# Halving the work pieces of rows 4 to 7 and re-cutting the last loads of a row-wise squared-distance kernel

## The chip, the cores and the metric

The kernel runs on one core of a Trainium2 chip. Times are device microseconds (us) of whole executions. A trace is one profiled execution; its span is some 1.9 us shorter than the time of the same execution (83.5 against 85.35 us for the profiled run before), and all positions below are microseconds from the start of the span.

## The reference

```python
batch, dim = 1024, 4096          # x, y: float32
def reference(x, y, axis):       # axis = -1
    return np.sum((x - y) ** 2, axis=axis).astype(np.float32)
```

## The kernel before

Each of the 128 partitions holds 8 rows of 4096 columns, so 32768 columns of x and as many of y pass through it. VectorE (DVE) subtracts in place, ScalarE (ACT) squares in place and sums along the columns through its accumulator. SyncE (SP) issues the loads. Buffers hold six rows; rows 6 and 7 come into the place of rows 0 and 1 and wait until those are squared.

The sizes of the loads (columns per partition; the late piece is the end of row 3, kept for the very last):

```python
xw = [16384, 8192, 5568, 1824, 512, 288]
yw = [16224, 8192, 2656, 2912, 928, 896, 512]
late, last = 160, 288
```

The loop runs over the y loads. A load is cut only at row borders, each piece is subtracted on VectorE and squared on ScalarE, and the piece that lands last is squared on VectorE itself:

```python
for j, (c0, c1) in enumerate(ys):
    final = j == len(ys) - 1
    wait_loaded(c1, landed_y[j][1])
    # ... pieces: [c0, c1) cut at multiples of D ...
    for piece in pieces:
        sub(*piece)                         # VectorE, X -= Y
        if final:
            # ... tensor_tensor_reduce on VectorE, starting from row 3's sum ...
            continue
        square(*piece, where[piece])        # ScalarE, waits for the subtraction
        # ... issue of rows 6 and 7 once rows 0 and 1 are squared ...
    if j == 4:
        complete(6)                         # VectorE adds the partial sums of row 6
complete(7)
```

## Time and profile before

| | before |
|---|---|
| time, median of 3 | 85.19 us (85.11 to 85.19) |
| span of the trace | 83.5 us |
| VectorE busy | 36.3 us, 18 instructions |
| ScalarE busy | 31.7 us, 27 instructions |
| loads | 15, 33.55 MB read, mean 402 GB/s |

The loads fill most of the span, so the kernel is near the pace of its data. The two compute engines look idle, at 44 and 38%, but that is an average: over 40 us they wait for the first large load, and in the last 10 us both are busy nearly all the time. The question for a change at the end of the kernel is which of the two, or which load, ends last there. The prediction shows the chain and the last instructions and reads them.

The group of subtractions and the group of squares, from the page of the kernel before (columns: line, engine, operation, output from input, shapes, count, then total busy us and mean ns of one, then idle time before them and what ended it):

```profile
L165 DVE TENSOR_TENSOR X<-X,Y 128x4096 f32<-128x4096 f32 (+9 forms) x14 | 35.8, 2593 | 45.2 <-DMA Y<-in_y_dram 45.1
L171 ACT ACTIVATE X<-X 128x4096 f32<-128x4096 f32 (+8 forms) x13 | 29.7, 2287 | 48.0 <-DVE X L165 48.0
L171 ACT ACTIVATION_READ_ACCUMULATOR X<-X 128x1 f32 x13 | 2.4, 186 | 0.0
```

ScalarE waits only for VectorE, VectorE only for loads, and every square has a second instruction of 186 ns behind it that reads the accumulator. Back to back, a square takes 0.185 us more than its columns (0.61 us for 512 columns, of which 0.427 are columns), so cutting squares in pieces is not free.

### The profile page before, as it was taken

Reading aid. Unit: us, or ns where it says so; the run is one execution under the profiler, and the core shown is the slowest. Engines: PE = TensorE matmul, PEld = TensorE weight load, DVE = VectorE, ACT = ScalarE, POOL = GpSimd, SP = SyncE. Lnnn points to the kernel's source line nnn. Section 1 sums busy time; section 2 is a strip of 40 time slices with the busy share of each in tenths; the row PEclk is TensorE's granted clock in tenths of the full one; section 3 lists DMA queues with packets and bytes.
Section 4 is the critical chain, followed back from the end, with each engine's and each line's share of the span. In section 5 each row is a group of like instructions: output and inputs, shape, how many; then the busy total and the mean of one; then the engine's idle time right before and its main releaser. Section 6 shows DMA issues by size and latency. Waiting matters only on the chain.

```text
span 83.5 us, 109 instructions
## 1 busy us (share of the span) xinstructions
DVE 36.3 (44%) x18; ACT 31.7 (38%) x27; POOL 0.2 (0%) x4
## 2 busy tenths in 40 slices
DVE  0000000000000000000299999999099995979980
ACT  0500000000000000000001979697970897989990
POOL 0000000000000000000000000000000000000000
DMA  9389999956999999589989998997999899999920
GB/s 471 157 377 502 502 502 502 471 251 283 497 497 497 497 497 404 218 373 497 439 377 439 487 439 345 487 487 330 423 437 437 378 443 427 423 407 410 394 66 2
DMA packets 2305, 33.56 MB, mean 402 GB/s; under 512 B 385, under 2 KB 769, under 8 KB 1409
## 3 DMA queue, kind: packets, MB, share of 16 engines
q1 hardware_dynamic: 2304, 33.56, 94.7%
q14 instruction: 1, 0.00, 0.0%
HBM read 33.55 MB, written 0.00 MB: 402 GB/s over the span
## 4 chain that ended last, share of the span: by engine, by line
DMA 68%; ACT 14%; DVE 14%; SPq 1%; issue 0%
DMA Y<-in_y_dram 68%; ACT X L171 14%; DVE X L165 14%; SPq L108 1%; DVE results L178 0%; SPq L215 0%
## 5 line engine op out<-in xcount | busy, mean ns | idle before, releaser
L165 DVE TENSOR_TENSOR X<-X,Y 128x4096 f32<-128x4096 f32 (+9 forms) x14 | 35.8, 2593 | 45.2 <-DMA Y<-in_y_dram 45.1
L171 ACT ACTIVATE X<-X 128x4096 f32<-128x4096 f32 (+8 forms) x13 | 29.7, 2287 | 48.0 <-DVE X L165 48.0
L171 ACT ACTIVATION_READ_ACCUMULATOR X<-X 128x1 f32 x13 | 2.4, 186 | 0.0
L171 ACT ACT_TABLE_LOAD x1 | 1.3, 1283 | 1.9 <-PEq L19 1.9
L178 DVE TENSOR_REDUCE results<-parts 128x1 f32<-128x2 f32 (+1 forms) x2 | 0.3, 152 | 0.2 <-ACT X L171 0.2
L199 DVE CUSTOM_DVE_ANT_0 Y<-X,parts 128x160 f32<-128x160 f32 x1 | 0.4, 385 | 0.0
L244 POOL MEMSET const-bfloat16-1.0<- 128x1 bf16 x1 | 0.1, 101 | 0.0
L244 POOL MEMSET const-uint8-127<- 128x1 uint8 x1 | 0.1, 101 | 0.0
L244 POOL MEMSET const-float32-0.0<- 128x1 f32 x1 | 0.1, 98 | 0.2 <-issue 0.2
L244 POOL MEMSET const-float32-1.0<- 128x1 f32 x1 | 0.1, 98 | 0.0
L199 DVE DVE_READ_ACCUMULATOR2_ANT results<- 128x1 f32 x1 | 0.1, 83 | 0.0
## 6 DMA issues: line engine op xcount, KB each, us to landing
Y<-in_y_dram SPq DMA_DIRECT2D x1, 8112.0 KB, 40.7
X<-in_x_dram SPq DMA_DIRECT2D x1, 4096.0 KB, 48.9
Y<-in_y_dram SPq DMA_DIRECT2D x1, 4096.0 KB, 58.3
X<-in_x_dram SPq DMA_DIRECT2D x1, 2784.0 KB, 13.4
Y<-in_y_dram SPq DMA_DIRECT2D x1, 1456.0 KB, 19.2
Y<-in_y_dram SPq DMA_DIRECT2D x1, 1328.0 KB, 16.2
X<-in_x_dram SPq DMA_DIRECT2D x1, 912.0 KB, 21.0
Y<-in_y_dram SPq DMA_DIRECT2D x1, 464.0 KB, 21.6
```

Of the source, the lines that this page charges most:

```text
L108: nc.sync.dma_start(out=dst[:, home(c0, c1)], in_=src[:, c0:c1]).then_inc(sem, 16)
L165: nc.vector.tensor_sub(out=a, in0=a, in1=Y[:, home(c0, c1)]).then_inc(diffs, 1)
L171: nc.scalar.activation(out=a, in_=a, func=Square, accum_out=acc).then_inc(acts, 1)
L178: nc.vector.tensor_reduce(out=results[:, r : r + 1], in_=parts_of(r, len(row_parts[r])), axis=mybir.AxisListType.X, op=add,).then_inc(sums, 1)
L199: nc.vector.tensor_tensor_reduce(out=Y[:, home(*piece)], in0=X[:, home(*piece)], in1=X[:, home(*piece)], scale=1.0, scalar=parts_of(r, 1), ...
L244: nc = _bacc.Bacc("TRN2", target_bir_lowering=False, num_devices=1)
```

## The change

The intent is to let ScalarE start on the first half of a piece while VectorE subtracts the second, and to bring the last data in smaller and more even portions. The edit, shortened where a line begins with @@, and without blank lines:

```diff
-    xw = [16384, 8192, 5568, 1824, 512, 288]
-    yw = [16224, 8192, 2656, 2912, 928, 896, 512]
-    late, last = 160, 288
+    xw = [16384, 8192, 5472, 1280, 960, 320, 160]
+    yw = [16256, 8192, 2624, 2784, 1344, 480, 480, 288]
+    late, last = 128, 192
     LATE = 3
+    halved = (1, 2, 3, 4)
@@ pieces are now cut by one function, used for the partial sums too @@
+    def pieces_of(j, c0, c1):
+        pieces = []
         while c0 < c1:
             e = min(c1, (c0 // D + 1) * D)
-            row_parts[c0 // D].append((c0, e))
+            if j in halved:
+                h = (c0 + e) // 64 * 32
+                pieces.append((c0, h))
+                c0 = h
+            pieces.append((c0, e))
             c0 = e
+        return pieces
@@ in the loop @@
         if j == 4:
-            complete(6)
+            for r in (4, 5, 6):
+                complete(r)
```

Load 1 is rows 4 and 5, load 2 the first 2624 columns of row 6, load 3 the next 2784 (the end of row 6 and the start of row 7), load 4 the next 1344; these four are halved per row. A row squared in several pieces has several partial sums, so rows 4 and 5 now need a `complete` of their own, a short reduction on VectorE.

More of the change, by code (lines that the diff above doesn't have):

```diff
@@ L127 @@
     row_parts = [[] for _ in range(R)]
-    for c0, c1 in ys:
+    def pieces_of(j, c0, c1):
+        pieces = []
         while c0 < c1:
             e = min(c1, (c0 // D + 1) * D)
-            row_parts[c0 // D].append((c0, e))
+            if j in halved:
[3 more added lines that the diff above has]
+            pieces.append((c0, e))
             c0 = e
+        return pieces
+    for j, (c0, c1) in enumerate(ys):
+        for piece in pieces_of(j, c0, c1):
+            row_parts[piece[0] // D].append(piece)
     parts, where = None, {}
@@ L188 @@
         wait_loaded(c1, landed_y[j][1])
-        pieces = []
-        while c0 < c1:
-            e = min(c1, (c0 // D + 1) * D)
-            pieces.append((c0, e))
-            c0 = e
-        for piece in pieces:
+        for piece in pieces_of(j, c0, c1):
             sub(*piece)
```

## The prediction

> **What bounds the kernel now.** I read the chain that ended last first, then the table of loads with their times to landing, then the last eight microseconds instruction by instruction, and the groups by shape for the cost of one instruction. The chain in order of time ends so:
>
> ```profile
> 54.11 16.24 DMA Y<-in_y_dram
> 70.35 0.02 issue
> 70.37 2.94 DVE X L165
> 73.31 0.02 issue
> 73.33 8.28 ACT X L171 x14
> 81.61 0.02 issue
> 81.64 0.16 DVE results L178
> ```
>
> Columns: start, duration, what. Up to 70.35 us the kernel waits for loads. From then on one whole subtraction (2.94 us, 2656 columns of row 6) lies on the chain, and behind it seven squares on ScalarE with their accumulator reads, back to back. So the end is not set by the last load but by a ScalarE that began row 6 late. The page's share of 68% for DMA hides this; the last 11 us are compute. The last instructions:
>
> ```profile
> 80.47 0.61 ACT L171 ACTIVATE X<-X 128x512 f32<-128x512 f32 x1
> 80.99 0.19 ACT L171 ACTIVATION_READ_ACCUMULATOR X<-X 128x1 f32 x1
> 81.02 0.39 DVE L199 CUSTOM_DVE_ANT_0 Y<-X,parts 128x160 f32<-128x160 f32 x1
> 81.08 0.43 ACT L171 ACTIVATE X<-X 128x288 f32<-128x288 f32 x1
> 81.33 0.08 DVE L199 DVE_READ_ACCUMULATOR2_ANT results<- 128x1 f32 x1
> 81.41 0.19 ACT L171 ACTIVATION_READ_ACCUMULATOR X<-X 128x1 f32 x1
> 81.64 0.16 DVE L178 TENSOR_REDUCE results<-parts 128x1 f32<-128x5 f32 x1 [0.23 <-ACT X L171]
> ```
>
> The last bracket is the point: VectorE waits 0.23 us for ScalarE before the final reduction. ScalarE's backlog is thus worth only about 0.2 to 0.3 us, because VectorE itself is done at 81.41. The loads (KB, us from issue to landing):
>
> ```profile
> Y<-in_y_dram SPq DMA_DIRECT2D x1, 1328.0 KB, 16.2
> ...
> Y<-in_y_dram SPq DMA_DIRECT2D x1, 464.0 KB, 21.6
> ...
> Y<-in_y_dram SPq DMA_DIRECT2D x1, 80.0 KB, 15.4
> ```
>
> With the issue times (54.11, 55.58, 65.07) these land at 70.3, 77.2 and 80.5. All landings after rows 4 and 5 (60.6) found in this way are 67.1, 70.3, 73.8, 76.1, 77.2, 78.2, 78.9, 79.5, 79.9, 80.3, 80.5 for 2784, 1328, 1456, 912, 464, 448, 256, 256, 144, 144 and 80 KB. A line through the steps between them gives 2.35 us per 1000 KB (436 GB/s) and 0.04 us per load, and meets every landing within 0.1 us. The queue does not run dry between the batches: the second batch is issued at 53.7, while the first runs to 60.6.
>
> **What the Trainium skill says.** "ScalarE: Activation LUTs", Rules for kernel authors, gives some 0.3 us per ACTIVATE and 0.83 ns per element. The trace agrees in slope (3617 ns for 4096 columns, 2417 for 2656: 0.833 ns), but back to back the fixed part is smaller: 512 columns go from 80.47 to the next start at 81.08, 0.61 us, less 0.427 is 0.185. "VectorE: DVE Perf Modes", Specifications and Mode 1×, gives one result per cycle at 0.96 GHz, 1.042 ns; the trace has (4421 - 2925)/1440 = 1.039 ns, with 0.155 us fixed, of which 0.08 overlap the next instruction, so 0.075 per extra subtraction. "DMA: Bandwidth & Descriptors", Bandwidth, calls transfers under 64 KB descriptor-dominated; the smallest new load is 64 KB, and here an 80 KB load behind others landed 0.2 us after its predecessor, so I price it by the fit. The same page, Queues, rings and completion order, has each DMA engine consume its ring in order; the landings above are in order of issue.
>
> **The change, part by part.** Nothing before 60.6 us changes except that the first y load has 32 columns (16 KB, 0.04 us) more, so the second batch is issued some 0.04 us later into a queue that is full anyway. The bytes are the same; there are 13 loads instead of 11 after the first four, two more at 0.04 us, so the last landing moves from 80.47 to about 80.5. By the fit the new landings that gate a subtraction are 70.2 (row 6, first 2624), 73.5 (2784), 76.7 (1344), 78.4 and 79.0 (480 each), 79.8 (288), 80.3 (192), 80.5 (128).
>
> Halves add six subtractions (rows 4 and 5 one each; one in 24576 to 27200; two in 27200 to 29984, which spans rows 6 and 7; one in 29984 to 31328), the new sizes one more (the last loads give 480, 480, 288, 192 where 896, 512, 288 were), and as many squares. On VectorE that is 7 x 0.075 = 0.5 us, nearly all in gaps that it waits out for loads. On ScalarE it is 7 x 0.185 = 1.3 us of work.
>
> What they buy is the lag. Row 5's last square starts after half a row: VectorE ends the four halves at 60.59 + 4 x 2.21 + 0.08 = 69.5, ScalarE squares the last 2048 columns in 1.71 + 0.185, so it is free at 71.4 instead of 73.1. Row 6's first 1312 columns are subtracted 70.20 to 71.72, the square starts at 71.76 (0.035 us from one engine to the other, as 73.29 to 73.33 now) instead of 73.33: 1.57 us earlier. From there the work left is 8192 columns as before, 6.83 us, but in 12 squares instead of 7: 12 x 0.185 = 2.22 instead of 1.30. Without any wait it would end at 71.76 + 9.05 = 80.81; so 0.92 of the 1.57 goes to fixed cost. Waits for subtractions come in between. Going through the pieces, each starting when its subtraction is done and the square before it is: 1312 at 71.76 and 73.20; 736 at 74.47 and 75.31; 640 at 76.10; 672 at 76.82, 77.59 and 78.37; 480 at 79.15 and 79.74; 288 at 80.34; 192 at 80.77, its accumulator read at 81.2. Now it is 81.60. The same rule, applied to the kernel before, gives 81.57, so it is good to some hundredths.
>
> VectorE: the two extra reductions (rows 4 and 5) cost 0.07 us each in pitch (78.23 to 78.30 now), beside the wait for the 480 columns. Then sub 192 at 80.34, sub 128 at 80.61 to 80.90, the squared sum 0.035 later to 81.29 (0.385 less 32 columns, plus the read), and the final reduction at 81.30 to 81.45, where it now ends at 81.80. Sum: -0.3 us. ScalarE, at 81.2, no longer holds the reduction; VectorE's own serial end after the last loads does. The store after it is unchanged.
>
> **The rivals.** First, the new sizes alone could be doing the work: the same walk with the new loads and no halves gives a reduction at 81.65, within 0.02 of now, and halves with the old sizes 81.75, slightly worse, for ScalarE then pays four more fixed costs and still meets the large 896 piece late. So neither pays alone; the pair does, which I believe because ScalarE is the bound in both. If ScalarE's fixed cost in small pieces is 0.21 and not 0.185, the gain shrinks to 0.2 us: 85.0.
>
> Second, DMA takes what is won: smaller loads (80, 96, 64 KB at the end, rows of 512 to 768 bytes) could each cost 0.1 rather than 0.04. Against it: the 80 KB load with rows of 640 bytes fits the line. If it came true, the end moves 0.2 to 0.3 us and the time is 85.1 to 85.2: nothing won. Related: the queue takes only a limited number of loads, the issue of the 144 KB y load took 4.87 us and the last 2.77. Two more loads mean that the last is issued only at some 71 to 74 us, still 5 us or more before its turn, so I count nothing.
>
> Third, the three reductions after the subtraction of 31328 hold VectorE if one of them waits for ScalarE: row 6's last square should end at 76.1, two microseconds before. If they did wait, VectorE would start the 480s late and all of it shift by that wait, to 85.2 or more.
>
> **Range and chances.** 85.19 - 0.3 = 84.88. The runs of before spread by 0.1%; the walk is good to 0.05, the landings to 0.1, and the rest of the range is small-load cost on the high side and on the low side a ScalarE that waits less or loads that land earlier. 84.6 to 85.15. Two per cent is 1.7 us: a gain of that size would need an end before the last load lands, so faster by 2% is out of reach; slower by 2% would need a stall of 1.7 us that nothing shows.
>
> **What would show it.** Right: last square's read ends before VectorE's last squared sum, the wait of the final reduction for ScalarE is gone or under 0.1; row 6's first square starts at about 71.8; the last y load lands at 80.5 +- 0.1; the final reduction starts near 81.3 and the span is 83.2. Wrong: last landing at 80.7 or later (the load rival), a wait of VectorE for ScalarE before the reductions of rows 4 to 6 (third rival), or ScalarE back to back into the final reduction (fixed cost mis-sized).

## The result

The changed kernel took 84.91 us (median of 4, 84.87 to 85.03) where the kernel before took 85.16 (median of 4). Ratios here and below are the mean time of one kernel's fast runs over the mean of the other's fast runs of the same rounds, so they are not quite the ratio of the medians: 0.9974, with a 95% interval of 0.9956 to 0.9991. It is a gain of 0.25 us where 0.3 was predicted.

The page of the changed kernel, busy times and the same groups:

```profile
DVE 36.8 (44%) x27; ACT 33.4 (40%) x41; POOL 0.2 (0%) x4
...
L177 DVE TENSOR_TENSOR X<-X,Y 128x2048 f32<-128x2048 f32 (+10 forms) x21 | 36.2, 1779 | 44.4 <-DMA Y<-in_y_dram 44.3
L183 ACT ACTIVATE X<-X 128x2048 f32<-128x2048 f32 (+9 forms) x20 | 31.2, 1560 | 45.8 <-DVE X L177 45.7
L183 ACT ACTIVATION_READ_ACCUMULATOR X<-X 128x1 f32 x20 | 3.7, 187 | 0.0
```

The kernel became faster while both engines became busier: seven more subtractions and squares, ScalarE 1.7 us more in busy time. What fell is ScalarE's wait for VectorE, from 48.0 to 45.7 us.

The chain of work that ended last, its end, in the changed kernel (start, duration, what; "issue" is time in which the engine waited for nothing that the profile shows, x2 that two instructions are merged):

```profile
67.52 12.66 DMA Y<-in_y_dram
80.19 0.02 issue
80.21 0.57 DVE X L177 x2
80.78 0.03 issue
80.81 0.35 DVE Y L206
81.16 0.01 DVE results L206
81.17 0.14 DVE results L190
```

Before, this chain left the loads at 70.35 us and ran 8.3 us on ScalarE. Now it stays with the loads until 80.19, the landing of the 192 columns, and has one microsecond of VectorE behind it. That landing only just decides: VectorE was busy with the 288 columns until 80.19 too, and waited 0.01 us for the 192 (0.07 and 0.09 in the other two traces of the change). ScalarE is gone from the end. The last instructions, in order of time:

```profile
80.67 0.35 ACT L183 ACTIVATE X<-X 128x192 f32<-128x192 f32 x1
80.81 0.35 DVE L206 CUSTOM_DVE_ANT_0 Y<-X,parts 128x128 f32<-128x128 f32 x1
80.92 0.19 ACT L183 ACTIVATION_READ_ACCUMULATOR X<-X 128x1 f32 x1
81.08 0.08 DVE L206 DVE_READ_ACCUMULATOR2_ANT results<- 128x1 f32 x1
81.14 0.16 DVE L190 TENSOR_REDUCE results<-parts 128x1 f32<-128x8 f32 x1
```

The final reduction has no bracket any more: it does not wait for ScalarE, whose last read ends at 81.11, before VectorE's own at 81.17. The margin is small: 0.06 us here, 0.08 and 0.09 in the other two traces. The reduction starts at 81.14 instead of 81.64. That is 0.5 us in these two traces, more than the 0.25 us of the clocked runs, because the first load happened to land 0.13 us earlier in this trace (41.01 against 41.14), and because single executions scatter: the profiled run before took 85.35 us, above all four clocked ones, and the one after 84.87. Counted from that landing, the final reduction starts after 40.13 us instead of 40.50, a gain of 0.37. This count, "first subtraction to final reduction", is used for all traces below. It takes out the spread of the first landing, though not that of the later ones, and it is one execution for each line of the table, so small differences are judged by the ratios.

### The profile page after: what moved, and what is told of

Read it like the earlier page. It is cut to its first block, busy times and chain, and to the rows that moved or that the text cites. A ratio compares the mean times of both kernels' runs of the same rounds, so it can differ in the third digit from the quotient of the medians.

```text
span 83.0 us, 135 instructions
## 1 busy us (share of the span) xinstructions
DVE 36.8 (44%) x27; ACT 33.4 (40%) x41; POOL 0.2 (0%) x4
## 4 chain that ended last, share of the span: by engine, by line
DMA 64%; SPq 17%; DVE 12%; ACT 4%; issue 1%
DMA Y<-in_y_dram 64%; SPq L109 17%; DVE X L177 11%; ACT X L183 4%; DVE Y L206 0%; DVE results L190 0%; SPq L222 0%; DVE results L206 0%
## 5 line engine op out<-in xcount | busy, mean ns | idle before, releaser
L177 DVE TENSOR_TENSOR X<-X,Y 128x2048 f32<-128x2048 f32 (+10 forms) x21 | 36.2, 1779 | 44.4 <-DMA Y<-in_y_dram 44.3
L183 ACT ACTIVATE X<-X 128x2048 f32<-128x2048 f32 (+9 forms) x20 | 31.2, 1560 | 45.8 <-DVE X L177 45.7
L183 ACT ACTIVATION_READ_ACCUMULATOR X<-X 128x1 f32 x20 | 3.7, 187 | 0.0
```

The lines of the kernel that those rows point to most:

```text
L177: nc.vector.tensor_sub(out=a, in0=a, in1=Y[:, home(c0, c1)]).then_inc(diffs, 1)
L183: nc.scalar.activation(out=a, in_=a, func=Square, accum_out=acc).then_inc(acts, 1)
```

## The experiments

My theory was that the end is a race between ScalarE's queue of squares and VectorE's short tail behind the last load, so that the parts do not add up: every place where ScalarE is late must be mended at once. The runs below come from three calls, each with its own runs of the kernel before. The rivals were that the load sizes do it (A), that the parts add up (B), that small loads cost more than the fit says (C), and that ScalarE has slack (D). All eleven runs gave correct results.

| run | ratio to before (95%) | first subtraction to final reduction | last wait of VectorE for ScalarE |
|---|---|---|---|
| before | 1 | 40.50 | 0.23 |
| the change | 0.9974 (0.9956 to 0.9991) | 40.13 | none |
| the change, second time | 0.9966 (0.9954 to 0.9977) | 40.11 | none |
| the change, third time | 0.9959 (0.9935 to 0.9983) | 40.13 | none |
| new sizes, no halves | 1.0014 (0.9995 to 1.0033) | 40.63 | 0.30 |
| halves, old sizes | 1.0005 (0.9993 to 1.0017) | 40.64 | 0.31 |
| no halves in rows 4, 5 | 1.0063 (1.005 to 1.0075) | 41.04 | 0.85 |
| halves in rows 4, 5 only | 1.0018 (1.0005 to 1.0032) | 40.51 | 0.32 |
| the 1344 whole | 1.0017 (1.0005 to 1.0029) | 40.54 | 0.40 |
| the 480s halved too | 1.0004 (0.9991 to 1.0016) | 40.44 | 0.31 |
| three x loads cut | 0.9992 (0.998 to 1.0004) | 40.41 | none |
| the same, second time | 0.9979 (0.9953 to 1.0005) | 40.40 | none |
| seven more x loads | 1.0015 (0.9988 to 1.0041) | 40.49 | none |

### New sizes, no halves

```diff
-    halved = (1, 2, 3, 4)
+    halved = ()
-            for r in (4, 5, 6):
+            for r in (6,):
```

> The new load sizes without any halves. My theory (the end is a race of ScalarE's queue of squares against VectorE's tail, and only the pair of sizes and halves takes ScalarE out of it): ScalarE starts row 6 a whole 2624-column subtraction late again and is back to back into the final reduction; time within 0.15 us of the kernel before (walk: +0.06, 85.2). Rival A (smaller last loads and earlier landings do the work, the halves are idle): 84.9, the whole gain. Rival B (each part adds its share): 85.0 to 85.05.

Measured: 85.35 us beside 85.25 of the kernel before, ratio 1.0014. Rivals A and B, which wanted 84.9 and some 85.0, fall. The chain of this run has the shape of the kernel before:

```profile
70.12 2.90 DVE X L177
73.03 0.02 issue
73.05 8.54 ACT X L183 x16
81.58 0.02 issue
81.61 0.16 DVE results L190
```

One whole subtraction, then sixteen instructions of ScalarE back to back into the final reduction. The last load is not in it.

### Halves with the old sizes

```diff
-    xw = [16384, 8192, 5472, 1280, 960, 320, 160]
-    yw = [16256, 8192, 2624, 2784, 1344, 480, 480, 288]
-    late, last = 128, 192
+    xw = [16384, 8192, 5568, 1824, 512, 288]
+    yw = [16224, 8192, 2656, 2912, 928, 896, 512]
+    late, last = 160, 288
```

> Halves of the same four loads, with the old sizes. My theory: ScalarE is early until the 896, 512 and 288 columns, which come in large lumps, and has paid four more fixed costs by then; it still holds the final reduction: 0.1 us slower than the kernel before (85.25), a wait of VectorE for ScalarE of about 0.3 us at the end. Rival A (the sizes do it): 85.15, no change. Rival B (halves alone carry the gain because the lag is what matters): 84.9.

Measured: 85.29 us, ratio 1.0005: no gain, which refutes rival B, and the final reduction waits 0.31 us for ScalarE. The interval also admits rival A's "no change" for this run, but A has fallen in the first. From the end of the chain:

```profile
78.56 1.01 DVE X L177
79.57 0.02 issue
79.60 2.09 ACT X L183 x6
81.69 0.02 issue
81.71 0.16 DVE results L190
```

ScalarE has caught up by 79.3, waits 0.28 us until the whole 896 columns are subtracted, and from 79.60 has 896, 512 and 288 to square while VectorE finishes. The expectation named this lump.

### No halves in rows 4 and 5

```diff
-    halved = (1, 2, 3, 4)
+    halved = (2, 3, 4)
-            for r in (4, 5, 6):
+            for r in (6,):
```

> The change with rows 4 and 5 whole again (halves only in the loads of rows 6 and 7). My theory: ScalarE is still squaring row 5 until 72.9, so the halves of row 6 wait behind it; they add fixed cost and save no wait: 0.6 us slower than the kernel before (85.75), 0.9 slower than the change, ScalarE back to back from row 4 to the end. Rival B (parts add up): two thirds or more of the gain remain, 84.95 to 85.0. Rival A: 84.9.

Measured: 85.81 us, ratio 1.0063, 0.56 us slower than the kernel before and 0.8 slower than the change. This is the sharpest run: taking away one of four helpful-looking parts leaves a kernel that is worse than with none. The chain and the last line of the trace:

```profile
69.24 12.77 ACT X L183 x26
82.02 0.02 issue
82.04 0.16 DVE results L190
```

```profile
82.04 0.16 DVE L190 TENSOR_REDUCE results<-parts 128x1 f32<-128x8 f32 x1 [0.85 <-ACT X L183]
```

ScalarE starts on row 5 at 69.24 and has no pause for the remaining 12.77 us. Halves of row 6 arrive while it is still busy with row 5, so they only add their fixed cost.

### Halves in rows 4 and 5 only

```diff
-    halved = (1, 2, 3, 4)
+    halved = (1,)
```

> The new sizes, and halves in rows 4 and 5 only. My theory: ScalarE is free at 71.4 but then waits for a whole 2624-column subtraction until 73.1, so the time won is idle time: within 0.15 us of the kernel before (walk +0.06, 85.2). Rival B (parts add up): a third or more of the gain, 85.0 to 85.1. Rival A (sizes): 84.9.

Measured: 85.38 us beside 85.26, ratio 1.0018. No gain; rival B's third of it is outside the interval. ScalarE in this trace:

```profile
71.20 0.19 ACT L183 ACTIVATION_READ_ACCUMULATOR X<-X 128x1 f32 x1
73.03 2.39 ACT L183 ACTIVATE X<-X 128x2624 f32<-128x2624 f32 x1 [1.65 <-DVE X L177]
```

It is free at 71.4, as it is in the changed kernel, and then sits idle for 1.65 us, until a whole subtraction of 2624 columns is done. The time won on row 5 is given back as a wait.

### The load of 1344 columns whole

```diff
-    halved = (1, 2, 3, 4)
+    halved = (1, 2, 3)
```

> The change with the one load of 1344 columns whole again. My theory: ScalarE is idle until the whole 1344 are subtracted (78.1) and then has 1344, 480, 480, 288, 192 in its queue, which ends 0.35 us after VectorE: the whole gain is lost, +0.09 against the kernel before (85.25), with a wait of VectorE for ScalarE of 0.3 us before the last reduction. Rival B (parts add up): a quarter of the gain lost, 84.95 to 85.0.

Measured: 85.38 us, ratio 1.0017: the whole gain is gone with one half, where rival B wanted a quarter of it gone. The trace shows ScalarE waiting in the middle and VectorE at the end:

```profile
78.30 1.32 ACT L183 ACTIVATE X<-X 128x1344 f32<-128x1344 f32 x1 [0.60 <-DVE X L177]
```

```profile
81.69 0.16 DVE L190 TENSOR_REDUCE results<-parts 128x1 f32<-128x7 f32 x1 [0.40 <-ACT X L183]
```

Loads 2 and 3 were not left whole one at a time. An estimate: a walk by the prediction's rules on the landings in the changed kernel's trace, which meets the four runs with the new sizes and other sets of halves to within 0.06 us, puts the final reduction some 0.9 us later with load 2 whole and 0.3 us later with load 3 whole.

### The two loads of 480 columns halved as well

```diff
-    halved = (1, 2, 3, 4)
+    halved = (1, 2, 3, 4, 5, 6)
```

> The change with the two loads of 480 columns halved as well: two more squares of 0.185 us fixed cost. My theory: ScalarE becomes the bound of the end again by 0.25 us: 85.15, the last reduction waits for it. Rival D (only VectorE's tail counts, ScalarE has slack): 84.9 to 84.95.

Measured: 85.25 us, ratio 1.0004, 0.1 us above what I expected and 0.3 above the change by the ratios. Rival D falls: in the change ScalarE is done only 0.06 to 0.09 us before VectorE, and two more fixed costs are 0.37; the final reduction waits 0.31. Its chain ends with ScalarE again:

```profile
73.11 8.34 ACT X L183 x26
81.45 0.02 issue
81.48 0.16 DVE results L190
```

### More loads of the same bytes

The first of these cuts three x loads in two, and was run twice. The second makes seven more loads.

```diff
-    xw = [16384, 8192, 5472, 1280, 960, 320, 160]
+    xw = [16384, 8192, 5472, 640, 640, 480, 480, 160, 160, 160]                               # three more
+    xw = [16384, 8192, 5472, 320, 320, 320, 320, 240, 240, 240, 240, 160, 160, 160]           # seven more
```

> The change with three x loads cut in two (1280, 960, 320), nothing else. My theory: a load in a full queue costs 0.04 us, so the last landing and the end move by 0.12 us: 85.0 (84.97 to 85.08). Rival C (a small load costs 0.1 us or more, or the queue's limit on loads in it delays the last ones): 85.2 or more.

> The kernel with three x loads cut in two, unaltered, to see whether the 0.1 us before its first cut load comes back. If it was the spread of one run: 0.14 us above the change, first row-6 load landing 9.65 us after rows 4 and 5. If the cut loads cause it through their issue or their place in the queue: 0.22 us above and 9.75 us again.

> The change with its x loads of 1280 and 960 columns cut in four each and that of 320 in two: seven more loads, same bytes. The run with three cuts was 0.22 us slower than the change, of which its trace shows 0.14 us (0.047 us a load) between the landing of the 2784-column y load and the last but one y load, and 0.1 us before the first cut load. Theory 'a fixed 0.047 us a load in the full queue': the stretch from the landing of the 2784 columns to that of the 192 grows from 6.77 to 7.1 us, the time is 0.33 us above the change. Rival 'some 0.07 us or more a load, once the queue's limit holds back the last issues': 0.5 us or more above the change.

Measured: 85.19 us for three more loads, and 85.12 in the repetition; 85.4 for seven more. By the ratios that is 0.22, 0.17 and 0.48 us above the change measured in the nearest or the same call. My first expectation (0.12 us) was too low. By time alone the seven-load run leans to the rival (0.5 or more), but its interval is 0.45 us wide, so I read the traces. The stretch from the first subtraction of the 2784-column load to that of the 192 columns, both within 0.03 us of a landing, is 6.78, 6.80 and 6.83 us in the three traces of the change, 6.93 and 7.00 with three more loads, and 7.15 with seven more. Against their mean of 6.80 that is 0.04, 0.07 and 0.05 us a load: a fixed cost, which does not grow with the number of loads, slightly above my 0.04. In these traces the rest of the 0.52 us between the seven-load run and the change of the same call is a first landing 0.16 us later (41.11 against 40.95). How much of the 0.48 us of the clocked runs is such spread is not shown.

One thing stays open. The first load of row 6 was taken up 9.75 and 9.71 us after rows 4 and 5 with three more loads, against 9.65 to 9.67 in the three traces of the change, before any cut load was due. It is no effect of many loads, since seven more gave 9.66, and the run with the new sizes and no halves, which cuts none of these loads, shows 9.72. That speaks for spread, but the repetition did bring most of it back, and nothing here settles it.

In all three VectorE has no wait for ScalarE at the end; more loads move the landings and the end moves with them. The chain of the seven-load run ends as that of the change does, with VectorE alone, 0.47 us later (its last two subtractions start at 80.68 instead of 80.21).

### The change repeated

These two runs are the unaltered changed kernel.

> The changed kernel again, unaltered, for the noise and the place of the first landing. My theory: 84.85 to 84.95; in its trace the first y load lands between 41.0 and 41.2 us, a spread from run to run that the change has no part in. Rival A' (the first y load's 32 more columns land earlier, by an effect of its size): first landing at 41.0 in every run with the new sizes and 41.14 with the old.

> The changed kernel once more, as the mark for the two others of this call: 0.9966 to 0.9974 of the kernel before, the 192 columns landing 6.77 us after the 2784.

Measured: 85.0 and 84.97 us, beside 85.25 and 85.26 of the kernel before, ratios 0.9966 and 0.9959. The first is slightly above the 84.85 to 84.95 that I expected, the second slightly faster than my 0.9966, and its 192 columns landed 6.83 us after the 2784 instead of 6.77. The gain is thus 0.2 to 0.35 us. The first y load was taken up at 41.01, 41.10 and 40.95 us in the three traces of the change, between 40.96 and 41.15 in the other traces with the new sizes, and at 41.14 and 41.07 in the two with the old sizes. Rival A', an effect of the first load's size, is not borne out: the spread of the new sizes covers the old.

No version beat the change.

## Why the prediction was right, point by point

**The bound before.** The step that named ScalarE's backlog and sized it at 0.2 to 0.3 us holds. All runs with the old sizes, or with one or more of the loads whole that the change halves, end with VectorE waiting 0.23 (the kernel before) to 0.85 us for ScalarE, and only the kernels with all four loads halved and the new sizes lose that wait (unless the 480s are halved too). One phrase is too strong: the last 11 us are not compute alone, since loads land until 80.47.

**The start of row 6.** The prediction put the first square of row 6 at 71.76; it was at 71.67, with rows 4 and 5 landing 0.15 earlier than before in that trace (60.44 against 60.59). ScalarE's fixed 0.185 us for a square was nearly right: squares of 480 columns start at 79.03 and 79.63, 0.60 us apart, of which 0.40 is the columns at 0.833 ns, which leaves 0.2; that is 0.015 more than assumed, and ScalarE still came in time. VectorE's 0.075 us for an extra subtraction holds too: half rows start 2.2 us apart, whole rows 4.34, so a cut costs 0.07. (Its fixed 0.155 goes with 1.042 ns a column; with the 1.039 beside it, 0.165 would be left.)

**The landings.** Predicted 80.3 for the 192 columns, measured 80.2. The last y load, predicted at 80.5 +- 0.1, landed at 80.37, 80.47 and 80.35 in the three traces of the change, twice just outside, in the traces whose first landing was 0.13 and 0.19 us earlier than before. It was issued at 70.4 to 70.5 (predicted 71 to 74), 10 us before it landed. The per-load cost of 0.04 us was a little low (0.04 to 0.07 in the runs with more loads). For two more loads that is at most 0.06 us of the sum, so it did not hurt.

**The three reductions.** They took 0.27 us together, 78.15 to 78.42, and waited for nothing; the third rival is not seen.

**The tail.** Predicted start of the final reduction 81.30, measured 81.14, 81.21 and 81.08 in the three traces of the change. Taken from the first landing, the walk's gain of 0.3 is 0.37 to 0.39 in the traces; in the clocked runs it is 0.2 to 0.35. The span was predicted at 83.2 and was 83.0 to 83.1.

**The rivals of the prediction.** The first was made of two numbers, final reductions at 81.65 for the sizes alone and 81.75 for halves with the old sizes. They were 81.61 and 81.71. That this is within 0.04 us is in part luck: counted from the first landing (41.14 in the prediction's kernel) they were predicted after 40.51 and 40.61 and came after 40.63 and 40.64, so the first is 0.12 late. The direction stands, since neither run was faster than the kernel before. The prediction therefore was right for its own reason: neither part pays alone. I had not predicted in advance that halving three of the four loads, without rows 4 and 5, is worse than halving none; that came out of the same walk when I wrote the expectation, and the chip agreed to within 0.1 us.

## What to carry to other kernels

When one engine hands pieces to another, cutting a piece in two pays only where the second engine is idle at that moment; where it has a queue, each cut adds its fixed cost (here 0.19 us a square) and wins nothing. So walk the last ten microseconds piece by piece, with the measured slope and fixed cost of each engine and the landings, and look for every place at which the follower waits: mending one place moves the wait to the next, and in this kernel the gain came only when the last was mended. Judge such a change by the chain of waits, as busy shares rise while the kernel becomes faster.

## What the Trainium skill lacked or had wrong

- "ScalarE: Activation LUTs": the page says that an ACTIVATE can give an accumulator output, but not that this brings a second instruction. Here every square has an accumulator read of 186 to 187 ns behind it. Its Rules for kernel authors give about 0.3 us per ACTIVATE, for a bias given as a pointer, plus 0.83 ns per element; the slope is right (0.833 ns here). The smaller fixed part measured back to back, 0.185 to 0.2 us, is no error of the page: under What ACT_TABLE_LOAD costs it has back-to-back ACTIVATEs overlap by about 93 ns, and here an accumulator read starts 0.09 us before the record of its square ends (80.99 against 81.08).
- "VectorE: DVE Perf Modes", The TRN2 errata, gives (N+151)/0.96 ns for an fp32 tensor_tensor, and calls it exact at 512 and 2048 columns. It holds at 4096 (4421 ns measured, 4424 by the formula); at 128 columns it is 2% high (285 measured, 291 by the formula).
- "DMA: Bandwidth & Descriptors", Bandwidth, gives 0.95 us for a 64 KB load, measured for loads issued by GpSimd. What it lacks is the cost of a small load behind others in SyncE's queue: the last 64 KB of the changed kernel landed 0.19 us after the load in front, and loads cut into pieces of 80 to 320 KB cost 0.04 to 0.07 us for each piece more (three and seven more loads). No load under 64 KB was run.
- No page I read says how many loads a queue takes before the issue of the next one is held up. Here most issue instructions took some 0.45 us each, but the ninth to twelfth of the second batch took 2.47, 4.78, 2.71 and 2.87 us (57.44 to 70.39). It delayed no landing that the traces show: the thirteenth was issued at 70.43 and landed at 80.37, right behind the twelfth.
